# Row-wise norm sums, marked pacing and a reordered last norm in a one-layer decoder step

## The chip, the cores and the metric

The kernel runs on one core of a Trainium2 chip. Each core has a matrix engine (PE in the profile, with PEld its weight loads), a vector engine (DVE), an activation engine (ACT), a general engine (POOL, also called GpSimd), and a sync engine (SP) that here only issues DMA transfers. Every engine takes its own instructions strictly in the order in which they were recorded and meets the others at semaphores, so an instruction that waits holds up all that stands behind it on its engine. DMA transfers run on 16 shared DMA engines and are issued from SP, ACT or POOL. The metric is the device time of one execution in microseconds; less is better.

## The reference

One decoder layer works on 320 tokens: a prompt of 256 and 8 samples of 8, with the same weights. All of it is float32.

```python
xn = rms_norm(x, g_mix)                     # mean of squares over 2048, per token
B, C, h, q, k, v, gate_c, gate_a = split(xn @ w_in)
y_conv = (B * dwconv3(C * h)) @ w_conv_out  # short causal convolution
y_attn = window_attention(q, k, v, rel_bias, sinks) @ w_attn_out
h = x + (sigmoid(gate_c) * y_conv + sigmoid(gate_a) * y_attn) @ w_o
hn = rms_norm(h, g_ffn)
h = h + (silu(hn @ w_gate) * (hn @ w_up)) @ w_down
y = rms_norm(h, g_final)
```

The keys, values and convolution rows of the last positions are returned too, so the sample caches are copied to outputs, shifted by eight positions.

## The kernel before, in words

**Tiling.** Activations stand transposed: 128 features on the partitions, 320 tokens along the row, 16 such chunks `k` for the 2048 features. Weights arrive in blocks of 512 KB, 128 partitions of 4 KB. To keep float32 accuracy on PE's faster number format, each block is split: ACT writes the rounded part (`whi`, line 97) and DVE writes what is left (`wlo`, line 98, raw minus rounded). The activations are split the same way (`xh_t`, `xl_t`; `hh_t`, `hl_t`). Each 128x128 tile of weights then costs three matrix products: high by high, high by low, low by high. `product` (line 109) does this for 256 output columns at a time, block by block; `kv_product` (line 277) does it for keys and values at the start, with x itself arriving at the same time; `down` (line 848) does the last matrix product in seven instead of eight block products by sums of weight blocks.

**Rings.** Raw blocks, high parts and low parts have 4, 3 and 3 buffers up to the output projection, and 6, 4 and 4 after it. SP issues the load of a block when the buffer's last reader is done. At the border (lines 774 to 778) the old pools are closed and new ones opened over the same memory, so the first new load waits for every last reader of the old pools.

**Stages in order.** `kv`; then `q`, `C`, `H`, `B` with the attention as side work; then eight rounds of `gc`, `ga` (gates), `yc` (convolution output) and `ya` (attention output); then `wo`; then three pieces of `fg`, `fu` (gate and up) each followed by two rounds of `down` (`P` and `Q` products; `na`, `nb` are the samples' share); the last piece also does the final norm as its columns become complete, and the last lines (997 to 1009) do what is left.

**Order of the work.** Python calls record the instructions, and a scheduler with its own idea of costs sets each engine's order. Side work is a generator: `tick` (line 104), after each block, lets it record one step, not ahead of the newest split and product. `pending` holds what is recorded after the next block's split.

**Norm sums.** The first norm's factor is per token, so it is applied after the products. `square_in` (line 260) lets POOL square each chunk of `hT` and add it into `hacc`; `root_of_sums` (line 268) sums over partitions with a product with ones, and computes the root on 128x320 tiles (`root_steps`, line 207). The same two functions serve the second norm at the border from `wo` to `fg`.

**Transfers beside the weights.** The weight sums that `down` needs are built in DRAM by 176 transfers of 512 KB from POOL's queue (`T<-...`, lines 179 and 181). Their pace: `sum_step` (line 171) first lets POOL copy two numbers out of the raw block that was last recorded, so the transfer is issued after that block has landed. Four cache copies of 480 KB (line 707) are paced the same way.

Of the kernel before, what the change touches and what calls it, by code (L numbers as in the profile page):

```python
# [44 lines left out]
def hybrid_layer(ctx: ExitStack, tc: tile.TileContext, a: dict, o: list):  # L45
# [34 lines left out]
    def tmp(tag, name):  # L80
        return wk[0].tile([P, UL], F32, tag=tag, name=u(name))
# [4 lines left out]
    def load_block(src, shape, behind=()):  # L86
# [3 lines left out]
        last["raw"] = raw  # L90
        hi, lo = ring_tile("whi", shape, F32R), ring_tile("wlo", shape, F32R)
        with after(*behind):
            split_to(hi[:, :n, :], lo[:, :n, :], raw[:, :n, :])
# [49 lines left out]
    pace = cst.tile([1, 2], F32, name="pace")  # L143
# [27 lines left out]
    def sum_step():  # L171
# [4 lines left out]
        p = nc.gpsimd.tensor_copy(pace, last["raw"][0:1, 0, 0:2])  # L176
# [25 lines left out]
    hacc = cst.tile([P, T], F32, name="hacc")  # L202
# [33 lines left out]

    sp = ExitStack()
# [22 lines left out]
    def square_in(kc, first):  # L260
        if first:
            nc.gpsimd.tensor_tensor(hacc, hT[:, kc, :], hT[:, kc, :], op=ALU.mult)
        else:
            t = tmp("tc", "sq")[:, :T]
            nc.gpsimd.tensor_tensor(t, hT[:, kc, :], hT[:, kc, :], op=ALU.mult)
            nc.gpsimd.tensor_tensor(hacc, hacc, t, op=ALU.add)

    def root_of_sums(out, v, s, r):
        pss = ps_aux(u("pss"))
        nc.tensor.matmul(pss[:, :T], ones, hacc, start=True, stop=True)  # L270
        nc.vector.tensor_scalar(v, pss[:, :T], 1.0 / D, EPS, op0=ALU.mult, op1=ALU.add)
        root_steps(v, s, r, out)
# [4 lines left out]
    def kv_product(tiles):  # L277
        ps = [ps_acc(u("kv")) for _ in range(4)]
        k0 = 0
        for i, n in enumerate(tiles):  # L280
# [9 lines left out]
            for k in range(k0, k0 + n):  # L290
                square_in(k, k == 0)
# [24 lines left out]

    def start_rest():
        yield
# [9 lines left out]
        yield  # L328
# [29 lines left out]
    pr_p = ExitStack()  # L358
    pr = pr_p.enter_context(tc.tile_pool(name="pr", bufs=1, side="right"))
# [24 lines left out]
    def bias_load(j, gp):  # L384
        bias = pr.tile([P, 2, 2, 2 * WIN], F32, tag="bias", name=u("bias"), bufs=2)
# [126 lines left out]
    def sample_attention(sm):  # L512
# [46 lines left out]
        for b in range(NB):  # L559
            nc.vector.tensor_scalar(s[:, b, :], s[:, b, :], den[:, b:b + 1], None, op0=ALU.mult)  # L560
# [48 lines left out]
    def kv_work():  # L609
        rt = zz.tile([P, 3, T], F32, name="rt")  # L610
        root_of_sums(rb, *(rt[:, i, :] for i in range(3)))
# [91 lines left out]
    def gate_work():  # L703
        for dst, src in cache_steps():
            p = nc.gpsimd.tensor_copy(pace, last["raw"][0:1, 0, 0:2])
            with after(p):
                nc.gpsimd.dma_start(dst, src)
            yield
# [387 lines left out]
```

## Time and profile before

| what | value |
|---|---|
| median of 3 runs | 1706.27 us (1704.98 to 1707.85) |
| the profiled execution | 1709.12 us, of which the span from first to last instruction is 1707.3 us |
| PE busy in the span | 1671.2 us (98%) |
| DVE, ACT, POOL busy | 1005.8, 710.6, 278.0 us |
| DMA moved | 385.68 MB, mean 226 GB/s |
| mean granted PE clock | 0.992 |

The page's part on waits says which engine's instruction ended another's idle time. A row of the timeline has its start and length in microseconds, the engine and line, what is written from what, and in brackets the idle time of that engine just before, with its releaser. Rows of the windows view give each engine's busy time in a stretch, and the granted PE clock as a share of the full one. Time in which PE neither works nor loads weights, and time in which it has a lower clock, is what separates the span from the products' own time.

### The profile page before, as it was taken

To read this page: it belongs to the slowest core of one execution; us is meant where nothing else is said; L and a number is where in the kernel's file an instruction comes from. 1 tells how busy PE (TensorE), PEld (TensorE's weight loads), DVE (VectorE), ACT (ScalarE), POOL (GpSimd) and SP (SyncE) were. 2 spreads that over 40 slices of the span, in tenths; PEclk is the share of its full clock that TensorE was granted. 3 is DMA by queue.
4 is the path that set the end of the run, shared out by engine and by line. 5 is a ranking of instruction groups with operands and counts; after the bars stand their busy time and mean duration, and the time that the engine had idled before them with its cause. 6 is when DMAs were issued, how large, how long until landed. Compare 5 with 4: busy or idle time off the path is not lost.

```text
span 1707.3 us, 26691 instructions
## 1 busy us (share of the span) xinstructions
PE 1671.2 (98%) x10674; PEld 1599.2 (94%) x10674; DVE 1005.8 (59%) x1368; ACT 710.6 (42%) x900; POOL 278.0 (16%) x507
## 2 busy tenths in 40 slices
PE   7999999999999999999999999999999999999996
PEld 6999999999999999998999988899999888999975
DVE  8558544344444445545555567755555687555687
ACT  4345333333333334434333345533333555333464
POOL 9001111121111124542111000011110000110000
PEclk9999999999999999999999999999999999999998
DMA  6554545688888889969777768898777788874575
GB/s 206 181 149 124 165 133 159 218 265 259 247 251 251 244 245 292 285 180 344 230 224 225 223 201 273 262 289 233 222 216 204 220 282 280 262 214 150 192 255 179
DMA packets 90715, 385.68 MB, mean 226 GB/s; under 512 B 12256, under 2 KB 12576, under 8 KB 83392
## 3 DMA queue, kind: packets, MB, share of 16 engines
q1 hardware_dynamic: 78064, 282.46, 49.3%
q0 software_dynamic: 12096, 100.84, 24.0%
q8 instruction: 83, 1.36, 0.3%
q10 hardware_dynamic: 432, 0.69, 0.1%
q14 instruction: 40, 0.33, 0.1%
HBM read 380.17 MB, written 97.48 MB: 280 GB/s over the span
## 4 chain that ended last, share of the span: by engine, by line
PE 94%; DVE 2%; ACT 1%; DMA 0%; POOL 0%; issue 0%; ACTq 0%; POOLq 0%
PE fg L121 18%; PE fu L121 18%; PE P L869 7%; PE ga L121 7%; PE gc L121 7%; PE wo L121 6%; PE Q L869 5%; PE yc L121 3%; PE C L121 3%; PE ya L121 3%; PE B L121 3%; PE q L121 3%; PE H L121 3%; PE na L875 2%; PE nb L875 2%; PE kv L298 1%
## 5 line engine op out<-in xcount | busy, mean ns | idle before, releaser
L98 DVE TENSOR_TENSOR wlo<-wraw,whi 128x1024 fp32r<-128x1024 f32 (+1 forms) x531 | 657.9, 1244 | 566.4 <-ACT whi L97 564.0
L97 ACT ACTIVATE whi<-wraw 128x1024 fp32r<-128x1024 f32 (+1 forms) x531 | 561.8, 1059 | 818.9 <-PE fu L121 158.4
L121 PE MATMUL fg<-hh_t,whi 128*128 128x320 f32 x704 | 218.4, 310 | 3.9 <-ACT whi L97 3.9
L176 POOL COPY pace<-wraw 1x2 f32<-1x2 f32 x176 | 62.4, 355 | 973.2 <-DMA wraw<-in_w_gate_dram 435.2
L121 PE MATMUL fg<-hl_t,whi 128*128 128x320 f32 x704 | 218.2, 310 | 0.0
L121 PE MATMUL fg<-hh_t,wlo 128*128 128x320 f32 x704 | 218.1, 310 | 0.0
L121 PE MATMUL fu<-hh_t,whi 128*128 128x320 f32 x704 | 217.2, 309 | 0.0
L121 PE MATMUL fu<-hl_t,whi 128*128 128x320 f32 x704 | 217.2, 309 | 0.0
L121 PE MATMUL fu<-hh_t,wlo 128*128 128x320 f32 x704 | 217.2, 309 | 0.0
L121 PEld LDWEIGHTS fg<-hh_t,whi 128*128 128x128 f32 x704 | 133.2, 189 | 4.5 <-ACT whi L97 4.4
L121 PEld LDWEIGHTS fg<-hl_t,whi 128*128 128x128 f32 x704 | 133.1, 189 | 0.1
L121 PEld LDWEIGHTS fg<-hh_t,wlo 128*128 128x128 f32 x704 | 132.9, 189 | 0.2 <-DVE wlo L98 0.2
L121 PEld LDWEIGHTS fu<-hh_t,whi 128*128 128x128 f32 x704 | 132.2, 188 | 0.0
L121 PEld LDWEIGHTS fu<-hl_t,whi 128*128 128x128 f32 x704 | 132.2, 188 | 0.0
L121 PEld LDWEIGHTS fu<-hh_t,wlo 128*128 128x128 f32 x704 | 132.2, 188 | 0.0
L121 PE MATMUL wo<-m_h,whi 128*128 128x320 f32 x256 | 79.9, 312 | 0.0
L121 PE MATMUL wo<-m_h,wlo 128*128 128x320 f32 x256 | 79.3, 310 | 0.0
L121 PE MATMUL wo<-m_l,whi 128*128 128x320 f32 x256 | 79.3, 310 | 0.0
L121 PE MATMUL ga<-xh_t,whi 128*128 128x320 f32 x256 | 79.0, 309 | 0.0
L121 PE MATMUL gc<-xh_t,whi 128*128 128x320 f32 x256 | 78.9, 308 | 0.0
L121 PE MATMUL gc<-xl_t,whi 128*128 128x320 f32 x256 | 78.9, 308 | 0.0
L121 PE MATMUL gc<-xh_t,wlo 128*128 128x320 f32 x256 | 78.9, 308 | 0.0
(290 smaller groups left out, 3459.9 us busy)
## 6 DMA issues: line engine op xcount, KB each, us to landing
T<-in_w_down_dram POOLq DMA_DIRECT2D x132, 512.0 KB, 6.7
wraw<-in_w_in_dram SPq DMA_DIRECT2D x128, 512.0 KB, 4.1
wraw<-in_w_gate_dram SPq DMA_DIRECT2D x88, 512.0 KB, 4.7
wraw<-in_w_up_dram SPq DMA_DIRECT2D x88, 512.0 KB, 4.8
wraw<-T SPq DMA_DIRECT2D x88, 512.0 KB, 4.4
wraw<-in_w_down_dram SPq DMA_DIRECT2D x66, 512.0 KB, 4.5
T<-T POOLq DMA_DIRECT2D x44, 512.0 KB, 5.2
wraw<-in_w_o_dram SPq DMA_DIRECT2D x32, 512.0 KB, 6.9
```

The source lines that it names most:

```text
L97: last["hi"] = nc.scalar.activation(hi, src, AF.Copy)
L98: last["lo"] = nc.vector.tensor_sub(lo, src, hi.bitcast(F32))
L121: last["mm"] = nc.tensor.matmul(ps[c][:, :T], w[:, k, c * P:(c + 1) * P], x(kc), start=(kc == 0 and i == 0), stop=(kc == nk - 1 and i == 2),)
L176: p = nc.gpsimd.tensor_copy(pace, last["raw"][0:1, 0, 0:2])
L298: last["mm"] = nc.tensor.matmul(ps[c][:, :T], w[:, k, c * P:(c + 1) * P], x(kc), start=(kc == 0 and m == 0), stop=(kc == KC - 1 and m == 2),)
L869: last["mm"] = nc.tensor.matmul(bank[prod], x, w[:, j, :], start=(first and m == 0), stop=(end and m == 2),)
L875: last["mm"] = nc.tensor.matmul(samp[side], sa[:, xv, kk, :], w[:, j, :], start=(first and m == 0 and prod == SHARED[side][0]), stop=(end ...
```

## The change

Six things are changed.

- **First norm's sums.** POOL's squares go. The kernel gets x a second time, with tokens on the partitions (`x_rows`), in six loads on POOL's queue (four of 512 KB, two of 256 KB) through two buffers. ACT squares each in place and sums along the row (`row_square`). They are side steps of `kv`.
- **Second norm's sums.** When `h_rows` has turned four chunks into rows, ACT squares those rows, three instructions per four chunks. The square writes into a scratch tile of the old pools, for the last four chunks into `usum`, which lies elsewhere.
- **The root.** `spread_root` computes it on 128x3 numbers, spreads them on three diagonal tiles, and three products with ones bring the factor to all partitions. Its steps are recorded over three ticks. At the second norm `feed_work` does this, and the weight sums go on after it.
- **Pace.** `at_pace` lets DVE copy one number of the newest low part into `marks`; POOL copies the mark and then issues the transfer. Cache copies and weight sums alternate over the first eight ticks, instead of four cache copies first.
- **Sample attention.** Eight multiplications by the reciprocal, one per sample, become one over all.
- **Final norm.** The products with `g_final` after `P6` are recorded after the last block's splits (`before_last`), and so is the samples' last part with its square, which came after the prompt's last rows before.

Where the scheduler's order differs is shown at three places.

ACT's instructions around the first round of gates, before. `whi_3294` is the high part of the first of `ga`'s four blocks, 3326 to 3388 are the others, 3428 and 3460 are `yc`'s two, 3492 the first of `ya`:

```order
L97 ACTIVATE whi_3294<-wraw_3292 128x1024
L731 ACT_TABLE_LOAD
L731 ACTIVATE gc_3284<-gc_3284 128x320
L731 ACTIVATE gc_3287<-gc_3287 128x320
L97 ACTIVATE cv_h<-bc_3137 128x320
L97 ACTIVATE cv_h<-bc_3142 128x320
L97 ACTIVATE whi_3326<-wraw_3324 128x1024
L97 ACTIVATE whi_3358<-wraw_3356 128x1024
L97 ACTIVATE whi_3388<-wraw_3386 128x1024
L731 ACTIVATE ga_3418<-ga_3418 128x320
L731 ACTIVATE ga_3421<-ga_3421 128x320
L97 ACTIVATE whi_3428<-wraw_3426 128x1024
```

The same place now; 3272 and 3305 are `ga`'s first two blocks, 3338 and 3371 the others, 3412 and 3445 are `yc`'s, 3482 is `ya`'s first:

```order
L97 ACTIVATE whi_3272<-wraw_3270 128x1024
L97 ACTIVATE whi_3305<-wraw_3303 128x1024
L748 ACT_TABLE_LOAD
L748 ACTIVATE gc_3262<-gc_3262 128x320
L748 ACTIVATE gc_3265<-gc_3265 128x320
L97 ACTIVATE whi_3338<-wraw_3336 128x1024
L97 ACTIVATE whi_3371<-wraw_3369 128x1024
L97 ACTIVATE whi_3412<-wraw_3410 128x1024
L97 ACTIVATE whi_3445<-wraw_3443 128x1024
L748 ACTIVATE ga_3402<-ga_3402 128x320
L97 ACTIVATE whi_3482<-wraw_3480 128x1024
L748 ACTIVATE ga_3405<-ga_3405 128x320
```

Both splits of `yc` now stand ahead of the sigmoids of `ga`, which wait for the end of `ga`'s products; before they stood behind them.

DVE's instructions in the sample attention beside the second `B` product, before. `s_s` are the samples' scores, `sden` the reciprocals, `cv` the convolution, and `wlo_2176` the low part for which `B` waits next:

```order
L558 RECIPROCAL sden<-sden 128x8
L560 TENSOR_SCALAR s_s<-s_s,sden 128x136
L673 SCALAR_TENSOR_TENSOR cv_2110<-ue_2103,vecs,cv_2110 128x336
L662 TENSOR_TENSOR ue_2116<-H_1929,csb_1926 128x256
L673 SCALAR_TENSOR_TENSOR cv_2110<-ue_2103,vecs,cv_2110 128x336
L663 TENSOR_TENSOR ue_2116<-H_1929,csb_1926 128x8x8
L560 TENSOR_SCALAR s_s<-s_s,sden 128x136 x4
L673 SCALAR_TENSOR_TENSOR cv_2123<-ue_2116,vecs,cv_2123 128x336
L560 TENSOR_SCALAR s_s<-s_s,sden 128x136
L673 SCALAR_TENSOR_TENSOR cv_2123<-ue_2116,vecs,cv_2123 128x336
L560 TENSOR_SCALAR s_s<-s_s,sden 128x136 x2
L98 TENSOR_TENSOR wlo_2176<-wraw_2173,whi_2175 128x1024
```

And now, with `wlo_2150` in its place:

```order
L575 RECIPROCAL sden<-sden 128x8
L576 TENSOR_TENSOR s_s<-s_s,sden 128x1088
L689 SCALAR_TENSOR_TENSOR cv_2091<-ue_2084,vecs,cv_2091 128x336
L678 TENSOR_TENSOR ue_2097<-H_1910,csb_1907 128x256
L689 SCALAR_TENSOR_TENSOR cv_2091<-ue_2084,vecs,cv_2091 128x336
L679 TENSOR_TENSOR ue_2097<-H_1910,csb_1907 128x8x8
L578 COPY pnew<-s_s 128x64
L98 TENSOR_TENSOR wlo_2150<-wraw_2147,whi_2149 128x1024
L689 SCALAR_TENSOR_TENSOR cv_2104<-ue_2097,vecs,cv_2104 128x336
```

Two of the four convolution steps moved behind the low part, and seven of the eight multiplications are gone from ahead of it.

DVE's last low part, before (`wlo_16145`; the rows of `hr` are prompt rows, `gt` holds `g_final`):

```order
L844 TENSOR_TENSOR hr<-hr,P_2090_16007 128x512
L932 TENSOR_TENSOR hr<-hr,gt 128x512 x2
L976 TENSOR_REDUCE rbsq<-rbsq 128x1
L98 TENSOR_TENSOR wlo_16145<-wraw_16142,whi_16144 128x1024
L977 TENSOR_SCALAR rbsq<-rbsq 128x1
L944 TENSOR_TENSOR hs<-hs,gt 64x512
```

And now (`wlo_16269`):

```order
L871 TENSOR_TENSOR hr<-hr,P_2075_16144 128x512
L98 TENSOR_TENSOR wlo_16269<-wraw_16266,whi_16268 128x1024
L965 TENSOR_TENSOR hr<-hr,gt 128x512
L1017 TENSOR_REDUCE rbsq<-rbsq 128x1
L965 TENSOR_TENSOR hr<-hr,gt 128x512
L1018 TENSOR_SCALAR rbsq<-rbsq 128x1
L977 TENSOR_TENSOR hs<-hs,gt 64x512
L873 TENSOR_TENSOR hr<-hr,Q_2094_16241 128x512
```

The two products with `g_final` moved from ahead of the last low part to behind it; the samples' square and product, which stood behind the second root, now follow the first.

In `kv`, where POOL's 31 squares and additions stood, POOL now has six loads, the first of them ahead of its small loads at the start and the second right behind those. On ACT the six row squares stand after the splits of the fourth, sixth (two of them follow it), eighth (two) and the first `q` block. At the border from `wo` to `fg`, ACT has three squares of `usum` between the last `hr` and `hs` copies and the first split of `fg`; the first load of `fg` now waits for no POOL instruction of the second norm, since the last reader of the old pools is a `wo` product.

The diff, cut to its core:

```diff
+    marks = cst.tile([1, 200], F32, name="marks")
+    def at_pace():
+        i = paced[0]
+        paced[0] += 1
+        nc.vector.tensor_copy(marks[:, i:i + 1], last["low"][0:1, 0, 0:1].bitcast(F32))
+        return nc.gpsimd.tensor_copy(pace, marks[:, i:i + 1])
...
-        p = nc.gpsimd.tensor_copy(pace, last["raw"][0:1, 0, 0:2])
+        p = at_pace()
...
-    def square_in(kc, first):
...
-    def root_of_sums(out, v, s, r):
...
+    def spread_root(ss, dg, out):
+        n = ss.shape[-1]
+        s3, v3, r3 = (dg[:, 3, i * 3:i * 3 + 3] for i in range(3))
+        nc.vector.tensor_reduce(s3, ss, axis=AX.X, op=ALU.add)
+        nc.vector.tensor_scalar(v3, s3, 1.0 / D, EPS, op0=ALU.mult, op1=ALU.add)
+        root_steps(v3, s3, r3, r3)
+        yield
+        for t, (t0, tn) in enumerate(TOK):
+            nc.vector.tensor_scalar(dg[:tn, t, :tn], ident[:tn, :tn], r3[:tn, t:t + 1], None, op0=ALU.mult)
+        yield
+        pb = ps_aux(u("pb"))
+        for t, (t0, tn) in enumerate(TOK):
+            nc.tensor.matmul(pb[:, t0:t0 + tn], ones[:tn, :], dg[:tn, t, :tn], start=True, stop=True)
+        nc.vector.tensor_copy(out, pb[:, :T])
...
-            for k in range(k0, k0 + n):
-                square_in(k, k == 0)
...
+    def row_square(i):
+        t, h = i // 2, i % 2
+        t0, tn = TOK[t]
+        xr = pr.tile([P, 1024], F32, tag="bias", name=u("xr"), bufs=2)
+        nc.gpsimd.dma_start(xr[:tn, :], a["x_rows"][t0:t0 + tn, h * 1024:(h + 1) * 1024])
+        nc.scalar.activation(xr[:tn, :], xr[:tn, :], AF.Square, accum_out=ssx[:tn, t, h:h + 1])
...
-        for b in range(NB):
-            nc.vector.tensor_scalar(s[:, b, :], s[:, b, :], den[:, b:b + 1], None, op0=ALU.mult)
+        nc.vector.tensor_tensor(s, s, den.unsqueeze(2).to_broadcast([P, NB, W2]), op=ALU.mult)
...
+            with after(at_pace()):
                 nc.gpsimd.dma_start(dst, src)
+            yield
+            sum_step()
             yield
...
+        if k % 4 == 3:
+            ns = slice((k - 3) * P, (k + 1) * P)
+            for t in range(3):
+                src = hr[:, t, ns] if t < 2 else hs[:64, ns]
+                n = src.shape[0]
+                nc.scalar.activation(
+                    (usum if k == KC - 1 else wk[0].tile([P, 512], F32, tag="junk", name=u("jk"), bufs=1))[:n],
+                    src, AF.Square,
+                    accum_out=ssx[:n, t, k // 4:k // 4 + 1],
+                )
...
+            if final and g == 1 and prods == ("Q4",):
+                before_last(n1, n2)
...
+        def before_last(n1, n2):
+            scaled(hr[:, 0, :], n2)
+            finish(0, hr[:, 0, :], y_p[0, 0:P, :], P, nc.sync)
+            scaled(hr[:, 1, :], n2)
+            sample_done(n1)
...
-    sample_done(slice(2 * SW, 3 * SW))
     finish(2, hs[:64, :], y_s.flatten_outer_dims(), 64, nc.sync)
```

More of the change, by code (lines that the diff above doesn't have):

```diff
@@ L89, in load_block @@
         nc.sync.dma_start(raw[:, :n, :], src.rearrange("p (k n) -> p k n", k=n))
-        last["raw"] = raw
         hi, lo = ring_tile("whi", shape, F32R), ring_tile("wlo", shape, F32R)
+        last["low"] = lo
         with after(*behind):
@@ L327, in start_rest @@
         nc.gpsimd.dma_start(e_scr, e_sb)
-        yield
+        for i in range(6):
+            yield
+            row_square(i)
         yield
@@ L609, in kv_work @@
     def kv_work():
-        rt = zz.tile([P, 3, T], F32, name="rt")
-        root_of_sums(rb, *(rt[:, i, :] for i in range(3)))
+        rt = zz.tile([P, 4, P], F32, name="rt")
+        yield from spread_root(ssx[:, :, 0:2], rt, rb)
         nc.vector.tensor_scalar(rbq, rb, HD ** -0.5, None, op0=ALU.mult)
@@ L704, in gate_work @@
         for dst, src in cache_steps():
-            p = nc.gpsimd.tensor_copy(pace, last["raw"][0:1, 0, 0:2])
-            with after(p):
+            with after(at_pace()):
                 nc.gpsimd.dma_start(dst, src)
+            yield
+            sum_step()
             yield
```

48 lines of the change are left out of this document (23 added, 25 removed).

## The prediction

> **What bounds the kernel now.** I read the page's busy times first, then PE's part of the waits, then the windows in which PE's granted clock is below 1.
>
> ```profile
> PE 1671.2 (98%) x10674; PEld 1599.2 (94%) x10674; DVE 1005.8 (59%) x1368; ACT 710.6 (42%) x900; POOL 278.0 (16%) x507
> ...
> PE kv L298 <- DVE wlo L98: 7.6, 4, 4.5
> PE fg L121 <- ACT whi L97: 3.9, 1, 3.9
> PE yc L121 <- ACT whi L97: 2.1, 1, 2.1
> PE B L121 <- DVE wlo L98: 2.0, 1, 2.0
> PE Q L869 <- DVE rbsq L977: 1.7, 1, 1.7
> ...
> PE pk L367 <- DVE vT L616: 0.6, 1, 0.6
> PE yc L121 <- DVE wlo L98: 0.4, 1, 0.4
> ```
>
> PE works 98% of the span. Only two things can be won while its products stay the same: these waits (total, times, longest, in us), and stretches at a lower clock. The rows below have start and end, length, each engine's busy time, the granted clock, DMA share and GB/s; DVE is the third engine, POOL the fifth.
>
> ```profile
> 6.50:13.36 6.86, 5.52 (x19) 5.12 (x20) 6.86 (x6) 5.85 (x11) 6.78 (x9) 1.00 1.01 351
> 204.50:207.91 3.41, 3.41 (x14) 3.41 (x15) 2.17 (x2) 0.00 (x0) 0.00 (x0) 0.50 0.67 221
> 337.62:341.03 3.41, 3.41 (x15) 3.41 (x14) 1.86 (x2) 0.23 (x1) 0.00 (x0) 0.50 0.97 235
> 771.12:777.94 6.82, 5.15 (x18) 4.93 (x19) 6.12 (x7) 4.23 (x4) 5.49 (x9) 0.50 1.04 375
> ```
>
> Three of them have half the clock, and each follows one of the waits listed. A full half-clock stretch of 3.41 us costs 1.7, so a wait costs more than its own length.
>
> **kv: POOL's squares go.** The pieces of the chain and one PE row carry the stage's length:
>
> ```profile
> 6.79 0.64 PE L298 MATMUL kv<-xh_t,whi 128*128 128x320 f32 x1 [1.16 <-ACT whi L97]
> ...
> 36.57 12.07 PE kv L298 x70
> 48.64 3.53 PE q L121 x24
> ```
>
> The stage runs from 6.79 to 48.64, 41.85 us. Its 192 products at q's pitch (3.53 / 24 = 0.147) would take 28.2. Until 13.36 the pitch is about 0.27 (two consecutive rows at half clock stand under B), though the clock row says 1.00 there: 24 products cost 0.12 more each, 2.9. The waits are 7.6. The last 70 took 12.07 instead of 10.3, 1.7 of lower clock. The remaining 1.4 are small waits. Why DVE is late:
>
> ```profile
> L254 DVE SCALAR_TENSOR_TENSOR xl_t<-hT,vecs,xh_t 128x320 fp32r<-128x320 f32 x16 | 18.2, 1180 | 4.7 <-ACT xh_t L253 4.7
> L98 DVE TENSOR_TENSOR wlo<-wraw,whi 128x1024 fp32r<-128x1024 f32 (+1 forms) x10 | 16.7, 1685 | 2.5 <-ACT whi L97 2.5
> L266 POOL TENSOR_TENSOR hacc<-hacc,sq 128x320 f32<-128x320 f32 x15 | 16.2, 1079 | 0.4
> ...
> L254 DVE SCALAR_TENSOR_TENSOR xl_t<-hT,vecs,xh_t x16: 537/1146/3640, 6.2 to 33.9; 128x320 fp32r<-128x320 f32 x16
> ...
> L98 DVE TENSOR_TENSOR wlo<-wraw,whi 128x1024 fp32r<-128x1024 f32 x64 | 78.8, 1232 | 79.6 <-ACT whi L97 79.5
> ```
>
> While POOL squares, DVE's `xl_t` takes 1180 ns in the mean, its shortest 537; a `wlo` takes 1685 against 1232 in the 256 us after the stage, where POOL does little. Without POOL the same work is 16 x 0.54 + 8 x 1.23 = 18.5 us, less than the products. So the 7.6 and the 1.7 should vanish. What comes instead is six `x_rows` loads, 2.56 MB, the first two ahead of the stage, where DMA already has share 1.01. At its 351 GB/s they cost 7.5 us if no part is hidden. The upper bound is that one more piece of the cold start goes, 12 in all. I allow 1.1 of small waits: later DMA has room, and ACT's squares stand behind splits that are early. kv then takes 28.2 + 2.9 + 1.1 = 32.2: **9.6 won** (2.1 to 12).
>
> **B.** What stands on DVE ahead of the low part that PE waits for:
>
> ```profile
> L560 DVE TENSOR_SCALAR s_s<-s_s,sden 128x136 f32<-128x136 f32 x8 | 3.0, 414 | 0.0
> L673 DVE SCALAR_TENSOR_TENSOR cv<-ue,vecs,cv 128x336 f32<-128x336 f32 x4 | 2.2, 558 | 0.0
> ...
> 202.95 1.34 DVE L98 TENSOR_TENSOR wlo<-wraw,whi 128x1024 fp32r<-128x1024 f32 x1
> ...
> 204.35 0.79 PE L121 MATMUL B<-xh_t,wlo 128*128 128x320 f32 x2 [2.00 <-DVE wlo L98]
> ...
> 205.21 0.47 PE L121 MATMUL B<-xl_t,whi 128*128 128x320 f32 x1
> 205.47 0.47 PE L121 MATMUL B<-xh_t,wlo 128*128 128x320 f32 x1
> ```
>
> Eight multiplications, 3.0, become one of 1088 elements, which I price by the 1232 ns of a two-input instruction of 1024: 1.3. Two `cv` steps, 1.1, move behind, and the small copy `pnew` moves ahead. The low part comes some 2.6 earlier, more than the 2.00 (2.2 with the pipeline's refill), and the half clock behind it, 1.7, has no cause left: **3.9** (1 to 3.9). The moved `cv` steps delay nothing that PE waits for soon.
>
> [...]
>
> **yc.** ACT's rows behind `ga`:
>
> ```profile
> 334.53 0.47 ACT L731 ACTIVATE ga<-ga 128x320 f32<-128x320 f32 x1 [1.00 <-DVE ga L730]
> 334.91 2.94 ACT L97 ACTIVATE whi<-wraw 128x1024 fp32r<-128x1024 f32 x3
> ```
>
> The split for `yc` starts at 334.91, only because it stands behind the two sigmoids, which wait for the last of `ga`. Now both splits of `yc` stand ahead. Gone: 2.1, 0.4 and the half clock of 1.7, **4.2** (0 to 4.7). Late next are the sigmoids, needed only when `yc` and `ya` are complete.
>
> **Border wo to fg.**
>
> ```profile
> 765.18 0.31 PE L121 MATMUL wo<-m_h,wlo 128*128 128x320 f32 x1
> ...
> 766.92 1.08 POOL hacc L266
> ...
> 768.02 3.55 DMA wraw<-in_w_gate_dram
> ...
> 771.68 2.26 ACT L97 ACTIVATE whi<-wraw 128x1024 fp32r<-128x1024 f32 x2 [1.79 <-DMA wraw<-in_w_gate_dram]
> ```
>
> The first load waited for POOL's last addition. Now its last predecessor is the `wo` product that ends at 765.5; issued then, it lands at 769.1. ACT meanwhile squares `usum` three times at 0.72 (a square with its read-out under the tail), behind copies that end about 767.2: free at 769.4. The split starts there, 2.3 earlier. PE idles less before it, and I take one half window where there were two (5.15 us of work at half clock lost 2.6; one loses 1.7): 0.9. **3.2** (1.5 to 4.9).
>
> **q.** The wait of `pk` goes, since DVE has no backlog from `kv`; three products with ones replace two. **0.6** (0 to 0.6).
>
> **Tail.** The chain at its end:
>
> ```profile
> 1690.46 1.20 DVE hr L932 x2
> ...
> 1691.73 1.13 DVE wlo L98
> ...
> 1692.94 1.19 PE Q L869 x4
> 1694.15 0.69 DVE hr L846
> ...
> 1694.93 0.72 ACT gt L929 x2
> ```
>
> Without the two products (1.20) ahead of it the last `wlo` ends 1.2 to 1.3 earlier, and so do PE's last four products, near 1692.8. But DVE then does the two products and the samples' addition, and is free for the last merge only about 1693.5 rather than 1694.15. The samples' square no longer stands behind the prompt's last root, so both roots come close together, and the last scaling ends about another 1.0 earlier: **1.6** (0.6 to 2.5).
>
> **At nothing:** 180 mark copies on DVE. Even at the 0.41 of an `s_s` step they are 74 us, against 701 us in which DVE is idle; the step behind them on DVE is a later low part. POOL's copies become shorter. The weight sums keep their number and bytes.
>
> **The sum** is 9.6 + 3.9 + 4.2 + 3.2 + 0.6 + 1.6 = 23.1, and 1709.1 becomes 1686.0. That profiled execution lies 2.85 above the median of the runs. 6.0 of the sum is clock (kv 1.7, B 1.7, yc 1.7, fg 0.9), and whether a gap costs a window depends on where the window's border falls; so against the median I count two thirds of it, 2.0 less. 1706.3 - 21.1 = 1685.2.
>
> **Rivals.**
>
> *The row loads eat kv's gain.* For: share 1.01 and 351 GB/s up to 13.36, and ACT takes its instructions in order, so a late `x_rows` load would hold up the splits behind its square. Against: the squares stand several splits back. Fully, 7.5 are lost: 1692.7.
>
> *Waits at B and yc move by one block instead of going.* For: both are orders on one engine, and ACT and DVE have the same amount of work there. Against: that work is far below PE's. Their 8.1, less the discount of 1.1 on their clock, is lost: 1692.2.
>
> *The change doesn't do what it says: DVE is slow in kv through the DMA's writes, not POOL.* For: DMA's share is 1.01 in the slowest piece. Against: the `wlo` of 204.50 to 207.91 beside a share of 0.67 are not slow (two in 2.17 us). kv's 9.6 is lost: 1694.8.
>
> *The half clocks behind B and yc have another cause and stay.* For: both waits, 2.0 and 2.1, are shorter than one window of 3.41, so a window can hold more work than idle time and still be followed by half clock. Against: they come directly behind these two waits, and nothing else distinguishes the places. The 3.4, of which 2.3 were counted, is lost: 1687.5. [...]
>
> *Slower: the new marks line the weight sums up against the loads.*
>
> ```profile
> wraw<-in_w_in_dram SPq DMA_DIRECT2D x57, 512.0 KB, 3.6
> ...
> T<-in_w_down_dram POOLq DMA_DIRECT2D x73, 512.0 KB, 7.0
> wraw<-in_w_in_dram SPq DMA_DIRECT2D x65, 512.0 KB, 5.5
> ```
>
> The first row is from 50 to 280 us, without the sums; the others from 280 to 768, with 94 of them (21 more are `T<-T`). A load takes 3.6 without them, 5.5 beside them. A sum is now released when a low part is written; that also frees a raw buffer, so a sum and a load start together. If the load got nothing until the sum (7.0) has landed, it would land at 10.6. Four raw buffers cover three blocks of 24 products, 10.6, less a split of 1.06: 9.5. Beyond that point PE waits for each load. At a quarter of the 1.1 excess, 0.3 for each of 94, 28 us: 1713. Against: the two queues shared the engines so far, and halfway between 5.5 and 10.6 is inside the cover.
>
> **Chances and range.** The forecast 0.53, the half clocks' stay 0.07, row loads 0.14, moved waits 0.12, DVE slow for another reason 0.04, marks 0.10. The likeliest case's own range is 1681 to 1689, from the terms' bounds that don't add up on one side. To 1697 it takes in all cases but the last; left out are the marks' case and some of the quick end of the first. About 0.2% is what a measurement of this kernel can tell. All cases but the marks' are faster by more than that, 0.90; the marks' case is slower at its price (0.07) or, with some twenty of the loads late, about the same (0.03).
>
> **What would show it.** kv: `xl_t` near 540 ns and `wlo` near 1230 between 5 and 40 us, no wait for `wlo` there, the first `q` near 39; else rival one (waits on `whi` or `x_rows`) or three (DVE as slow as now). B and yc: no PE wait over 0.5 us there, and no half clock behind. Border: the first gate load issued as the last `wo` product ends, some 2.5 us earlier in the stage than now, the split directly behind the `usum` squares. Tail: some 0.4 of wait before the last `Q`, both roots together. Marks: loads between 280 and 768 landing in 5 to 7 us, and no PE wait on `whi` there; a landing beyond 9.5 would make the prediction wrong.

## The result, and the profile after

The changed kernel takes 1692.89 us in the median (1692.52 to 1693.66), against 1706.59 for the kernel before on the same chip: a ratio of 0.9921, with a 95% interval of 0.9904 to 0.9938. It is 13.7 us faster; 21 were forecast, 1685.2 in a range of 1681 to 1697. So the direction and the range held, and the likeliest value was 7.7 too low, near the rival "the row loads eat kv's gain" (1692.7).

The page and PE's part of the waits of the changed kernel (total, times, longest, in us; line numbers are those of the changed kernel from here on, unless it is said otherwise):

```profile
PE 1665.8 (99%) x10682; PEld 1593.4 (94%) x10682; DVE 991.5 (59%) x1553; ACT 724.0 (43%) x936; POOL 203.0 (12%) x451
...
PE kv L308 <- ACT whi L97: 4.5, 3, 1.9
PE fg L121 <- ACT whi L97: 3.8, 1, 3.8
...
PE kv L308 <- DVE wlo L98: 0.7, 1, 0.7
PE q L121 <- ACT kT L361: 0.4, 1, 0.4
PE Q L896 <- DVE wlo L98: 0.4, 1, 0.4
```

The waits of B, yc and pk are gone. kv's wait for `wlo` fell from 7.6 to 0.7, but a wait for `whi` of 4.5 stands in its place (1.4 of it before the first product, where it was 1.2), and the wait at the border is still 3.8.

The first products of the stages, read from the groups of both traces, show where the 16.2 us between the two profiled spans (1707.3 and 1691.1) came from. Each term is the difference that its stage adds:

| stage | up to | before | changed | the stage adds | predicted |
|---|---|---|---|---|---|
| kv | first q | 48.48 | 42.66 | 5.8 | 9.6 |
| q | first C | 106.81 | 100.72 | 0.3 | 0.6 |
| B | first gc | 305.0 | 295.1 | 3.7 | 3.9 |
| yc | first ya | 345.36 | 330.34 | 5.2 | 4.2 |
| border, and fg's first products | first fu | 789.40 | 772.78 | 1.6 | 3.2 |
| P and Q products | last P | 1687.2 | 1671.8 | -1.2 | 0 |
| tail | end of span | 1707.3 | 1691.1 | 0.8 | 1.6 |
| sum | | | | 16.2 | 23.1 |

Of these 16.2, 13.7 are left between the medians: 2.5 are the distance of the profiled execution of before from its median, for which 2.0 had been taken off.

DVE's rows between 5 and 44 us show that POOL no longer holds it up: `xl_t`, at 1180 ns before, is at 535, and `wlo`, at 1685, is at 1122.

```profile
L98 DVE TENSOR_TENSOR wlo<-wraw,whi 128x1024 fp32r<-128x1024 f32 (+1 forms) x11 | 12.3, 1122 | 11.0 <-ACT whi L97 11.0
...
L265 DVE SCALAR_TENSOR_TENSOR xl_t<-hT,vecs,xh_t 128x320 fp32r<-128x320 f32 x16 | 8.0, 535 | 6.3 <-ACT xh_t L264 6.2
```

**kv.** Two windows (start and end, length, busy time of PE, PEld, DVE, ACT, POOL, granted clock, DMA share, GB/s), then ACT's timeline:

```profile
9.38:12.79 3.41, 1.53 (x12) 1.26 (x10) 1.07 (x3) 1.92 (x3) 0.00 (x0) 1.00 0.98 348
12.79:16.20 3.41, 3.41 (x12) 3.17 (x13) 2.35 (x4) 1.97 (x3) 0.00 (x0) 0.50 1.04 414
```

```profile
11.64 1.06 ACT L97 ACTIVATE whi<-wraw 128x1024 fp32r<-128x1024 f32 x1 [1.41 <-DMA wraw<-in_w_kv_dram]
...
28.30 1.06 ACT L332 ACTIVATE xr<-xr 128x1024 f32<-128x1024 f32 x1 [4.39 <-DMA xr<-in_x_rows_dram]
...
29.35 1.04 ACT L97 ACTIVATE whi<-wraw 128x1024 fp32r<-128x1024 f32 x1
```

The split at 11.64 waits for a block of kv's weights while DMA is full (share 0.98). Two row loads share it there: in e1 and e6 below, which have none at the start, the same split comes at 8.85 and 9.04. PE then works only 1.53 of 3.41 us, and a half-clock window follows. At 28.30 ACT, which takes its instructions in order, has stood 4.39 us before a row square whose load was late, and the next split stands behind it. The chain of waits shows why that load was late (start, length, what):

```profile
19.57 0.52 POOL e_scr L343
20.08 8.13 DMA xr<-in_x_rows_dram
...
28.30 0.09 ACT xr L332
...
31.70 9.61 PE kv L308 x64
41.31 0.95 ACT whi L97
...
42.66 10.80 PE q L121 x72
```

POOL issued it only behind the small transfer `e_scr`. And `q`'s first split (41.31) stands behind the last row square and the root's table load.

**Border.** The chain at the same place as in the prediction:

```profile
753.67 0.57 ACT usum L784
...
754.30 1.05 ACT whi L97
...
755.40 16.65 PE fg L121 x96
772.05 0.81 PE pb L283 x6
```

The split starts directly behind the squares of `usum`, as predicted. But the 96 products take 16.65 us where 14.1 would do at full clock (at q's pitch of 0.147), and the products of the root, 0.81, now stand between `fg` and `fu`, while their counterparts of before lay in the gap between `wo` and `fg`.

**Tail.** The samples' two stores land last. SP's timeline in the changed kernel has the first of them at 1684.19, in the kernel before at 1701.82. Their rows in the view of DMA issues (count, KB each, median us from issue to landing), of the changed kernel and then of the kernel before:

```profile
out_dram<-hs SPq DMA_DIRECT2D x2, 256.0 KB, 4.6
```

```profile
out_dram<-hs SPq DMA_DIRECT2D x2, 256.0 KB, 3.3
```

From the start of the last P product on high parts alone (1671.8 and 1687.2) to the first of these stores it is 12.4 us now and was 14.6: that store's scaling ends 2.2 earlier. But the span gains only 0.8: all stores now come within 4.3 us (1680.7 to 1685.0) instead of 6.1 and the last ones take 4.6 us instead of 3.3. In e9 below, where the old order spreads the stores over 6.1 us again, they take 3.3 too.

### The profile page after: what moved, and what is told of

Read it like the earlier page. It is cut to its first block, busy times and chain, and to the rows that moved or that the text cites. A ratio compares the mean times of both kernels' runs of the same rounds, so it can differ in the third digit from the quotient of the medians.

```text
span 1691.1 us, 26865 instructions
## 1 busy us (share of the span) xinstructions
PE 1665.8 (99%) x10682; PEld 1593.4 (94%) x10682; DVE 991.5 (59%) x1553; ACT 724.0 (43%) x936; POOL 203.0 (12%) x451
## 4 chain that ended last, share of the span: by engine, by line
PE 96%; DVE 1%; DMA 1%; issue 1%; ACT 0%; POOL 0%; DVEq 0%; ACTq 0%; POOLq 0%
PE fg L121 18%; PE fu L121 18%; PE P L896 7%; PE wo L121 7%; PE gc L121 7%; PE ga L121 7%; PE Q L896 5%; PE C L121 3%; PE B L121 3%; PE H L121 3%; PE q L121 3%; PE yc L121 3%; PE ya L121 3%; PE na L902 2%; PE nb L902 2%; DMA xr<-in_x_rows_dram 1%
## 5 line engine op out<-in xcount | busy, mean ns | idle before, releaser
L98 DVE TENSOR_TENSOR wlo<-wraw,whi 128x1024 fp32r<-128x1024 f32 (+1 forms) x531 | 647.4, 1223 | 572.2 <-ACT whi L97 570.3
L151 POOL COPY pace<-marks 1x1 f32<-1x1 f32 x180 | 35.8, 199 | 1045.2 <-DVE marks L150 1045.1
L121 PE MATMUL ga<-xl_t,whi 128*128 128x320 f32 x256 | 79.1, 309 | 0.0
```

Of the source, the lines that this page charges most:

```text
L98: last["lo"] = nc.vector.tensor_sub(lo, src, hi.bitcast(F32))
L121: last["mm"] = nc.tensor.matmul(ps[c][:, :T], w[:, k, c * P:(c + 1) * P], x(kc), start=(kc == 0 and i == 0), stop=(kc == nk - 1 and i == 2),)
L151: return nc.gpsimd.tensor_copy(pace, marks[:, i:i + 1])
```

## The experiments

A first product's time is read from the group views; the median of each kernel is given beside that of the changed kernel on the same chip, 1692.10 (e0), where no other is named. e3, e8, e9 and e11 ran on another chip, on which the kernel before took 1707.30; beside e0 it took 1707.43. Executions of one kernel spread over 0.6 to 3.6 us (lowest to highest), those of the kernel before over 5.4 (1704.65 to 1710.07 in ten) and, on the other chip, over 5.9 (in eleven).

### The changed kernel again

> The changed kernel once more, on the chip of these runs, as their reference: 1692.5 to 1693.7 if the chip makes no difference.

1692.10 (1691.73 to 1694.38), ratio 0.9910 (0.9898 to 0.9922), 0.4 below the expected range. Its profile shows what sets the start of `q`. PE waits 2.06 us until 12.70, much as in the first profile, but a border divides the wait between two windows (0.98 and 1.48 us of idle time), and no half clock follows. Yet `q` starts at 42.34, only 0.3 earlier, because PE then waits longer for `kT`, which ACT writes behind the last row square and the root:

```profile
PE q L121 <- ACT kT L361: 1.6, 1, 1.6
```

ACT stands 3.40 us there for the load of that square, which POOL issued at 31.60, when the buffer of an earlier square came free. So it is the end of the row path that sets the start of `q` here, more than the waits ahead of it. In the profiles of e3, e4, e8 and e9, which keep the row path in `kv`, PE's wait for `kT` is 1.1 to 1.4.

### e1: no row sums

```diff
         for i in range(6):
             yield
-            row_square(i)
```

> The changed kernel without the first norm's row sums (no loads of x_rows, no squares; the factor comes from a constant instead, so this part of the computation is left out). Theory L: the row loads and squares cost kv the 3.6 us that are missing from its gain. Then q's first product comes at 38.5 to 39.5 us instead of 42.7, no wait for whi at 12.8 and 30.4, and the time is 3 to 4 us below the changed kernel, about 1689.3. Rival K: kv's own loads starve PE now that it has the full clock from its first product on. Then the wait at 12.8 and the half clock behind it stay, q starts at 41 or later, and the time is within 1.5 us of the changed kernel.

1687.35 (1686.98 to 1687.57): 4.8 below e0, 5.5 below the first runs. `q` starts at 37.52 instead of 42.66, and kv's only wait is the one ahead of its first product:

```profile
PE kv L308 <- ACT whi L97: 1.4, 1, 1.4
```

Theory L holds, with a larger price than it said: the row path costs 5.1 us of kv. Rival K is not tested by this profile alone, since the clock was half until 10.8 in it. It is out by e6's: there the full clock is granted from 5.2 on, no row load runs at the start, and kv has no wait for `whi` but the one ahead of its first product.

### e7: before, without POOL's squares

```diff
-            for k in range(k0, k0 + n):
-                square_in(k, k == 0)
+            if k0 == 0:
+                nc.vector.memset(hacc, 16.0)
```

> The kernel before with POOL's 31 squares and additions for the first norm taken out and nothing in their place (the sums are set to a constant, so this part of the computation is left out). PE, ACT and SP keep their order, DVE has one small memset more. Theory P: the squares alone cause kv's waits for wlo. Then xl_t takes 0.54 and wlo 1.2 us, the waits of 7.6 us are gone, q starts at 37.5 to 40.5 instead of 48.6, and the time is 8 to 11 us below the kernel before. Theory E: the squares cost what they cost in e2, 1 to 2 us, and the rest of kv's loss before comes from the clock and the order. Then q starts at 44 or later and the time is at most 4 below.

1696.43 (1695.13 to 1697.13) against 1707.43 for the kernel before: 11.0 less, `q` starts at 37.36 instead of 48.48. The groups between 5 and 44 us:

```profile
L98 DVE TENSOR_TENSOR wlo<-wraw,whi 128x1024 fp32r<-128x1024 f32 (+1 forms) x13 | 14.8, 1137 | 7.6 <-ACT whi L97 7.6
...
L254 DVE SCALAR_TENSOR_TENSOR xl_t<-hT,vecs,xh_t 128x320 fp32r<-128x320 f32 x16 | 7.8, 532 | 4.8 <-ACT xh_t L253 4.6
```

`xl_t` is at 532 ns, the waits for `wlo` are gone. Theory P holds at its upper end: in the order of the kernel before, POOL's squares alone cost 11 us.

### e2 and e11: the squares put back

e2 is e1 with the 31 instructions back on POOL. In e11 POOL's `e_scr` moves behind them:

```diff
+            for k in range(k0, k0 + n):
+                spare_square(k, k == 0)
...
-        nc.gpsimd.dma_start(e_scr, e_sb)
         for i in range(6):
             yield
+        with after(last["add"]):
+            nc.gpsimd.dma_start(e_scr, e_sb)
```

> The kernel of e1 with POOL's 31 squares and additions put back beside kv as spare work that nobody reads; the order of PE, ACT, DVE and SP is the same as in e1. Theory P: POOL slows DVE. Then xl_t has a mean of 1.1 to 1.2 us instead of 0.54, wlo 1.6 instead of 1.2, q starts at 46 to 49 us, and the time is 8 to 10 us above e1. Rival D: DMA's writes slow DVE. Then xl_t stays at 0.54 and the time is that of e1.

1689.44 (1688.17 to 1690.91), 2.1 above e1; `q` starts at 38.76. Both theories missed: DVE was slower (`xl_t` 676 ns, `wlo` 1453), but the cost was a quarter of theory P's. The timeline of POOL in e2 shows what was different:

```profile
12.91 1.84 POOL L277 TENSOR_TENSOR spare<-spare,sq 128x320 f32<-128x320 f32 x1
18.21 0.52 POOL L354 DMA_DIRECT2D e_scr<-e_sb  x1 [3.46 <-DVE e_sb L353]
18.74 7.02 POOL L277 TENSOR_TENSOR spare<-spare,sq 128x320 f32<-128x320 f32 x1
```

POOL stopped for 3.46 us, and the addition behind it took 7.02, during which DVE ran at its full pace (1.20 for a `wlo`). It is POOL that was held up there, and since nothing waits for these squares, the last of them slid behind the stage (to 50 us). e11 takes that stop away and touches nothing but POOL's order.

> e2 with POOL's small transfer e_scr and what depends on it moved behind the squares, so that POOL no longer stops 3.5 us for e_sb among them; the other engines' order is that of e2. Theory H: where both run without a pause each of DVE and POOL slows the other, and in e2 it was that stop which let DVE get ahead (it ran at full pace from 14.4 to 25 us while one addition on POOL took 7.0). Then xl_t's mean is back at 1.0 to 1.2 us, q starts at 44 to 49 and the time is 6 to 11 us above e1's 1687.4. Rival O: the squares cost little whenever PE and the splits run in the changed kernel's order; then q starts at 39 to 40 and the time is that of e2, 1689.4, within 1.5.

1693.52 (1691.19 to 1694.13): 6.2 above e1, 4.1 above e2, with PE, ACT, DVE and SP in the same order. `q` starts at 43.14, a little earlier than theory H said:

```profile
L277 POOL TENSOR_TENSOR spare<-spare,sq 128x320 f32<-128x320 f32 x15 | 20.2, 1347 | 0.6
L98 DVE TENSOR_TENSOR wlo<-wraw,whi 128x1024 fp32r<-128x1024 f32 (+1 forms) x11 | 16.6, 1526 | 1.1 <-ACT whi L97 1.1
...
L265 DVE SCALAR_TENSOR_TENSOR xl_t<-hT,vecs,xh_t 128x320 fp32r<-128x320 f32 x16 | 15.6, 1017 | 4.9 <-ACT xh_t L264 4.9
```

Theory H holds: `xl_t` is back at 1017 ns. Of the 4.4 by which `q` starts later than in e2, about 1.6 are, by an estimate from the half-clock stretches, the clock of the start (half until 13.5 here; in e2 full from 5.2 to 8.6 and from 12.1 on), and e11 ran on the other chip. The same squares cost 2, 6 or 11 us. A stop of POOL made the difference between 2 and 6; why it is 11 and not 6 in the kernel before was not tried.

### e5 and e6: the row sums later

```diff
     def kv_work():
+        for i in range(0, 6, 2):
+            row_square(i)
+            row_square(i + 1)
+            yield
         yield from spread_root(ssx[:, :, 0:2], rt, rb)
```

with `q`'s first output formed as soon as the factor is there. In e6 the loads are held back as well:

```diff
+        for i in range(0, 6, 2):
+            with after(at_pace()):
+                xr = row_load(i), row_load(i + 1)
+            yield
+            row_square(i, xr[0])
+            row_square(i + 1, xr[1])
+        yield
```

> The changed kernel with the six row squares recorded beside the first two q products instead of beside kv, and the root behind them; the first two x_rows loads still stand at the start. Theory A, ACT's order: kv loses because splits stand behind a square that waits for its load (30.4 us) and behind the last square and the root (42.6). Then q starts at about 40.5 and the time is about 2 below the changed kernel. Theory S, the start: kv loses mainly because the first two row loads take their share of DMA before 12 us. Then the wait at 12.8 stays and q starts at about 41.5 to 42, and the time is at most 1 below.

1690.34 (1688.94 to 1690.97), 1.8 below e0; `q` starts at 38.95, 3.7 earlier than in the changed kernel. Theory A holds; `q` starts even earlier than the 40.5 that it said. The start's wait for `whi` shrank to 0.3, though the two row loads still stand there: in that execution the first products ran at half clock (until 10.5) and so the next block, whose split came at 11.55, was hardly missed.

> As e5, and the x_rows loads are held back by marks until q's first blocks, two at a time, with each pair of squares one block behind its loads. Theory L: what the row path costs is its loads at the start and its squares between kv's splits. Then q starts at 37.5 to 38.2, as in e1, and the time is 1687.5 to 1689, up to 2 below e5. Rival: the loads beside q's weights delay these, ACT stands at a square that waits, and PE waits for whi in q by as much as kv has won; then the time is that of e5 or more.

1688.87 (1688.28 to 1690.65), 1.5 below e5, with ranges that overlap, and 3.2 below e0, ratio to before 0.9892 (0.9879 to 0.9906). `q` starts at 36.10, 1.4 before e1's, which had half the clock until 10.8 where e6 had it in full. But `q` itself takes 59.9 us, 2.0 more than in e1; 1.4 of that are two waits, which the rival named:

```profile
PE q L121 <- DVE wlo L98: 0.7, 1, 0.7
PE q L121 <- ACT whi L97: 0.7, 1, 0.7
```

### e4 and e10: spare products at the border

```diff
+    def bridge():
+        fill = ps_aux("fill")
+        for _ in range(6):
+            nc.tensor.matmul(fill[:, :T], ones, rb, start=True, stop=True)
+    pending.append(bridge)
     mp_.close()
     early.close()
```

> The changed kernel with six spare products of 128x320 (0.54 us each at full clock) on PE in the gap between wo and fg, 3.2 us of the 3.8; the order of the other engines is the same. Theory C: the half clock at the start of fg comes from PE's idle time before it, though that is a wait of little more than one window of 3.41 us that covers parts of two. Then both half windows go, the 96 products up to fu take about 15 us instead of 17.4, and the time is 2.0 to 2.6 us below the changed kernel. Rival: the clock falls for another reason; then the time is the same, or 0.5 above if the spare products end late.

1691.63 (1690.98 to 1694.62), 0.5 below e0 and 1.3 below the first runs. The windows around the gap in the changed kernel (first three) and in e4:

```profile
750.07:753.49 3.42, 1.30 (x9) 0.76 (x8) 1.42 (x3) 2.60 (x9) 0.00 (x0) 1.00 0.41 143
753.49:756.90 3.41, 1.50 (x5) 1.28 (x6) 1.52 (x2) 2.94 (x7) 0.00 (x0) 0.50 1.03 416
756.90:760.31 3.41, 3.41 (x14) 3.41 (x15) 3.04 (x9) 3.38 (x4) 0.00 (x0) 0.50 1.02 412
```

```profile
751.63:755.05 3.42, 2.81 (x11) 1.67 (x9) 0.24 (x2) 3.31 (x9) 0.00 (x0) 1.00 0.92 358
755.05:758.46 3.41, 3.00 (x18) 2.73 (x19) 2.69 (x4) 1.95 (x2) 0.00 (x0) 1.00 1.02 411
```

With spare work in the gap PE idles for 0.61 and 0.41 us in the two windows of e4, against 2.12 and 1.91 in the first two of the changed kernel, and the half clock is gone. Nothing else on PE was changed, so in this case it hung on PE's idle time. From the last `wo` product to `fu` the trace is 1.55 us shorter (1.97 at `fu` less 0.42 that it had before); two small waits, 0.6 and 0.4, show that the splits now are what fg waits for. That is less than the 2.0 to 2.6 expected, and the medians do not resolve it: 0.5 to 1.3.

> e6 and the six spare products of e4 in the gap between wo and fg. If both savings are independent, the time is that of e6 less 1.3 to 2.0 us, about 1686.5. Rival: the spare products save a clock window in one phase of the windows only; then it is less than 0.7 below e6.

1688.33 (1686.73 to 1689.23), ratio 0.9885 (0.9872 to 0.9899): 0.5 below e6, with ranges that overlap, so by the medians it is the rival's "less than 0.7", and the two savings together are not shown to add. By the traces the stretch from the end of `wo` to `fu` is 1.9 shorter than in e6 (20.65 against 22.51), but `q` starts 1.1 later, in an execution with half the clock until 10.1. It has the lowest median of the whole kernels here, 3.8 below e0.

### e3: eight multiplications

```diff
-        nc.vector.tensor_tensor(s, s, den.unsqueeze(2).to_broadcast([P, NB, W2]), op=ALU.mult)
+        for b in range(NB):
+            nc.vector.tensor_scalar(s[:, b, :], s[:, b, :], den[:, b:b + 1], None, op0=ALU.mult)
```

> The changed kernel with the eight multiplications by the reciprocal back in place of the one; all eight and the four cv steps stand ahead of the low part again. As predicted: PE waits about 2 us for it in B, and a half-clock window of 1.7 follows in part of the executions only (in e7 the wait was there without it): 2.2 to 3.9 us above the changed kernel's 1692.1 to 1692.9, about 1695. Rival: the step that held up DVE was another one; then there is no PE wait in B and the time is the same within 0.7.

1695.32 (1694.09 to 1696.87), 3.2 above e0. The wait is back with its old length (the scheduler puts all four convolution steps ahead of the low part again, too), and the prediction's step for B is confirmed:

```profile
PE B L121 <- DVE wlo L98: 2.0, 1, 2.0
```

In this profile no half clock follows. The wait falls into two windows, where in the kernel before it lay in one (e3's two windows, then that of before and the one behind it):

```profile
193.36:196.77 3.41, 2.66 (x19) 2.40 (x17) 3.41 (x10) 1.68 (x3) 2.23 (x7) 1.00 0.00 0
196.77:200.18 3.41, 2.14 (x14) 2.15 (x15) 3.41 (x4) 0.00 (x0) 1.27 (x3) 1.00 0.31 96
```

```profile
201.09:204.50 3.41, 1.42 (x10) 1.15 (x9) 3.41 (x8) 1.06 (x1) 2.14 (x4) 1.00 0.00 0
204.50:207.91 3.41, 3.41 (x14) 3.41 (x15) 2.17 (x2) 0.00 (x0) 0.00 (x0) 0.50 0.67 221
```

### e8: paced by raw blocks

```diff
-        nc.vector.tensor_copy(marks[:, i:i + 1], last["low"][0:1, 0, 0:1].bitcast(F32))
-        return nc.gpsimd.tensor_copy(pace, marks[:, i:i + 1])
+        return nc.gpsimd.tensor_copy(pace, last["raw"][0:1, 0, 0:1])
```

> The changed kernel with its transfers paced by one number of the newest raw block again, without marks and without DVE's 180 copies; the scheduler then puts both ga sigmoids ahead of the second split of yc again, as before. Theory M: the marks matter only through that order. Then loads between 270 and 760 land in 5 to 6 us as in the changed kernel, and the time is above it by what comes back at yc, 0.5 to 4.2 us. Rival: the marks keep transfers and loads apart; then waits for whi appear at many places and the time is 5 us or more above. If the marks are pure cost, the time is below by up to 1.

1697.64 (1697.28 to 1698.82), 5.5 above e0. Loads land as quickly as in the changed kernel (the 65 of `w_in` between 270 and 760 us in 5.2 us in both), and waits do not appear at many places but at one (PE's timeline, then ACT's):

```profile
339.38 0.42 PE L121 MATMUL gc<-xh_t,whi 128*128 128x320 f32 x1 [2.83 <-ACT whi L97]
```

```profile
337.92 0.47 ACT L97 ACTIVATE m_h<-ga 128x320 fp32r<-128x320 f32 x1 [1.27 <-DVE ga L754]
338.29 2.94 ACT L97 ACTIVATE whi<-wraw 128x1024 fp32r<-128x1024 f32 x3
```

ACT holds the split for the second round's `gc` behind the two roundings of `m_h`, which wait for the end of `ya`: the stall of yc, one round's step later. Theory M holds in kind (the order, not the transfers), at a price of 5.5 where it said 0.5 to 4.2, and not at the place that it named; by the trace 5.3 of it lie between 322 and 356 us, half clock included. The rival of distributed waits is out.

### e9: the old tail

```diff
-            if final and g == 1 and prods == ("Q4",):
-                before_last(n1, n2)
...
-                if g == 0:
-                    scaled(hr[:, 0, :], n2)
-                    scaled(hr[:, 1, :], n2)
+                scaled(hr[:, 0, :], n2)
+                scaled(hr[:, 1, :], n2)
+                if g == 1:
+                    finish(0, hr[:, 0, :], y_p[0, 0:P, :], P, nc.sync)
...
+    sample_done(slice(2 * SW, 3 * SW))
     finish(2, hs[:64, :], y_s.flatten_outer_dims(), 64, nc.sync)
```

> The changed kernel with the end of the final norm in the old order: the two products with g_final and the first rows' scaling right after P6, the samples' last part behind the second prompt rows. As predicted the new order is worth 1.6 us, as the two traces put it 0.8 (from the last P product to the end). So the time is 0.8 to 1.6 above the changed kernel. Rival: what the last low part wins, the products behind it on DVE lose; then the time is the same within 0.4.

1693.05 (1692.45 to 1694.24), on another chip than e0: 0.2 above the first runs and 0.95 above e0, which does not settle it. Between the two profiled executions it is 0.8: `fu` starts 0.93 earlier in e9 than in the changed kernel, and the spans are 1691.0 and 1691.1. The wait for the last low part is back (1.6 us).

## Why the prediction was right or wrong

**kv, 9.6 predicted, 5.8 measured: the one large miss.** Its first half, "POOL's squares go", was right: 10.7 without the allowance for waits, 11.0 measured (e7). The step that failed is the next one, "I allow 1.1 of small waits: later DMA has room, and ACT's squares stand behind splits that are early". The row path costs 5.1 (e1), between the 1.1 and the 7.5 that the loads would take at the measured 351 GB/s. The reasons given for 1.1 fail one by one: DMA had no room at the start (share 0.98 from 9.38 to 12.79), a square stood 4.39 us for a load that POOL had issued late, and the last square and the root's table load stood ahead of `q`'s first split and of `kT`. Moving squares and loads behind kv returns 3.2 of it (e6).

A second error hid part of the first: the sum kept 2.9 for a cold start until 13.4, but in the changed kernel's profile the full clock is granted from 6.0 on. That is not the change's doing; the start was slow in some profiles of both families: full clock came at 13.4 and 4.3 in the two of the kernel before (e7 is the second), between 4.8 and 13.5 in those of the changed one.

**B, 3.9 and 3.7: right**, and e3 shows that the eight multiplications were the cause, with the convolution steps that the scheduler puts among them. The clock's 1.7 in it hangs on where the wait lies, so that its lasting value is 2.2 to 3.2.

**yc, 4.2 and 5.2: right in mechanism**, 1.0 more: before, `yc` started 2.9 later behind `ga` than it does now, and `ya` another 2.3 later; the sum had 2.1 and 0.4 of waits and 1.7 of clock. What the prediction did not see is why the order changed: e8 has no marks and gets a stall of the same kind. So "at nothing" for the marks was wrong in effect. No cost of theirs shows and they keep no transfer from a load, but the order that the scheduler finds with them is worth 5.5 us.

**Border, 3.2 and 1.6.** The load and the split came 2.4 earlier (2.3 predicted). Two terms failed. "One half window where there were two", 0.9, did not come, since 2.1 and 1.9 us of idle time lay in two successive windows. In e0's execution it did come, and the stretch from the end of `wo` to `fu` was still only 0.4 shorter (21.9 against 22.3, before 23.9): `fg`'s first four products ran at the full clock, but PE then waited 0.3 for the low part, and the product with it started 1.3 behind `fg`'s first in both. And the root's products, for which the prediction has no term at this border, cost 0.8, because they left the gap and now stand between `fg` and `fu`.

**Tail, 1.6 and 0.8.** PE's wait and the last merge went as said (the merge 0.7 earlier against the last P product, 0.65 predicted), and the scaling of the samples ends 2.2 earlier, more than the 1.6. The sum stopped there and took the stores behind them as unchanged; 1.4 of it was lost to stores that now come closer together and land later.

**Q and P products, 0 and -1.2: not foreseen.** Their distance is 233.4 ns in all kernels built from the changed one, 232.4 in the two built from the one before. e8, without marks, has it too. The cause was not tried and stays open.

**Rivals.** The row loads ate 5.1 of the 7.5 that rival gave them: it was under-rated at 0.14. (Its price, 1692.7, counts the 7.5 on top of the 1.1 that the sum already holds; 1691.6 would be consistent.) That the time fell near this price is partly luck, since border, tail and the P and Q products added their own shortfall of 3.6. "DVE is slow in kv through the DMA's writes" is out (e7: DMA's loads stay, `xl_t` falls to 532 ns). "Waits move by one block" did not happen in the changed kernel, but it is what e8 does. The half clocks behind B and yc did not stay: in the changed kernel's profile, without these waits, the clock is full from 16.21 to 753.49 us. The marks' case is out: loads of `w_in` land in 5.2 us, before it was 5.5.

**The discount for the median**, 2.0, came out near: 2.5. The two thirds in it were the author's estimate, which no run shows. The reason is borne out in part: in the profiles of e3 and e7 the wait in B, 2.0 us, is there without a half clock. That the 2.5 themselves come from such windows is not shown; the profiled execution of before also had half the clock until 13.4.

## What to carry to other kernels

Work that is moved off a contended engine must be followed to all that it now passes through: here a transfer queue, a full DMA and an engine that takes its instructions in order gave back half of what the move won. A term that "lies beside other work" should be priced by the stage in which it lands, and an unknown between 1.1 and 7.5 should not be taken at its low end when the profile shows DMA at share 1.01 there. Where a scheduler sets the order, a change that costs nothing can move a stall: look at each place where an engine in order puts an instruction that waits for the end of a product ahead of the next product's split.

## What the runs showed of the hardware

**Half clock behind idle time of PE.** The shortest half-clock stretches in the traces of the kernel before and of the changed one last 3.41 us (204.50 to 207.91 and 12.79 to 16.20), and the stretches at full clock between two changes are whole multiples of 3.413 (737.28 us, from 16.21 to 753.49 in the changed kernel, is 216 of them; 163.84, from 40.66 to 204.50 in the kernel before, 48). In windows of this length, counted from the changes, PE's idle time ahead of a half-clock window was 2.73, 2.00, 2.20 and 2.61 us in the kernel before (windows from 33.84, 201.09, 334.21 and 767.70) and 1.88 and 2.12 in the changed one (from 9.38 and 750.07). Behind these two kernels' other full-clock windows, up to the tail, the clock stayed full; they had at most 1.77 (before, from 30.42) and 1.28 (changed, from 29.86). That is no sharp limit: over all fourteen profiles windows with 1.64 to 1.77 us went either way. A half-clock window with 1.67 us of idle time (before, from 771.12) and one with 1.91 (changed, from 753.49) were followed by another one, in e11 one with 0.29 was too, and those without idle time from 774.53 (before) and 756.90 (changed) were followed by full clock.

The wait of 2.00 us in B of the kernel before lay in one such window, and a half-clock window, 1.7 us of work, followed; in e3 a border divided it, with 0.75 and 1.27 us of idle time on its two sides, and none did. Executions of one kernel differ by this: in the changed kernel a wait of 1.88 near 12 us was followed by half clock, in e0 a wait of 2.06 was not. The spread of the kernel before, 5.4 us, against 2.7 for the changed one (e0) goes with its longer list of waits of 2 us; that this is the reason is argued, not shown.

**DVE and POOL beside each other in `kv`.** In e11, where both worked almost without pause (10.65 and 10.49 of the 10.65 us from 14.35 to 25.00), each took longer: POOL's additions 1347 ns in the mean, of which the quickest took 874, and DVE's `xl_t` 1017 and `wlo` 1526, against 532 and 1137 in e7 without the squares. But in e2, where DVE was ahead with work in a row, one addition on POOL took 7.02 us, while four `xl_t` on DVE took 1.92 together and a `wlo` 1.20 (1.22 in the mean of the whole changed kernel): DVE lost nothing. Between e2 and e11 only POOL's order differs, so its stop of 3.5 us decided which of the two paid.
